# A macaron encoder trunk on one core: merged gate/up exits, P of two head groups through DRAM, a fourth seven-product chunk, and q, k ahead of V

## The chip, the cores and the metric

The kernel runs on one core of a Trainium2 chip. The metric is the device time of one execution in microseconds (us), from the first to the last activity on the core. Beside it stand views of one profiled execution of the kernel before. The engines are the tensor engine (PE, with its weight loads shown as PEld), the vector engine (DVE), the scalar engine (ACT), GpSimd (POOL) and the sync engine (SP), which here only issues DMAs.

## The reference

The input x is 256 rows (frames) of 1024. Two layers follow each other, and each is three residual blocks:

```python
for i in range(DEPTH):                                  # 2
    h = rmsnorm(x, ffn1_norm[i])
    x = x + 0.5 * swiglu(h, ffn1_w_gate[i], ffn1_w_up[i], ffn1_w_down[i])      # 1024 -> 2816 -> 1024
    h = rmsnorm(x, mix_norm[i]); proj = h @ w_in[i]     # q_s, k_s, v_s (768 each), q_m (256)
    ...                                                 # attention, see below
    x = x + concatenate([o_s, o_m]) @ w_out[i]
    h = rmsnorm(x, ffn2_norm[i])
    x = x + 0.5 * swiglu(h, ffn2_w_gate[i], ffn2_w_up[i], ffn2_w_down[i])
```

with swiglu(h) = (silu(h @ w_gate) * (h @ w_up)) @ w_down. In layer 0, o_s is causal chunked attention of 12 heads of 64 with a learned relative bias (chunks of 64 frames, and with 256 frames every earlier chunk is in reach). In layer 1 it is differential attention of 6 heads, softmax(q1 k1) - lambda softmax(q2 k2), with rotary embedding and a norm of the result. o_m is 4-head attention into a memory of 256 rows. q and k of every head are normalised. All data are float32.

## The kernel before

**Tiling.** Rows are two blocks tb of 128; features lie in tiles of 128. A product runs on the tensor engine as three matmuls of a rounded and a rest part (float32r): hi x hi, hi x lo, lo x hi (`dense`, lines 555, 558, 561). So each weight chunk is loaded by DMA into a raw buffer of 128 x 2048, ACT writes hi (L378, a cast) and the vector engine lo = raw - hi (L398). There are 3 raw buffers and 4 hi/lo buffers, so weights are split some chunks ahead.

**Stages.** FFN 1, mixer, FFN 2 of layer 0, then of layer 1. In an FFN the 2816 hidden columns are 11 groups of 256; a group needs two weight chunks (g, c), and its gate and up columns share one PSUM bank of 512 for each tb. `evac` ends a group: silu on ACT (L741), a multiply (L744) and a 32 x 32 block transpose (L752) on the vector engine, for each tb; then hb goes to DRAM and comes back re-ordered as hr, and is split into hi and lo (ht). Two groups of each FFN (`PAIR`) are computed as a pair by seven block products instead of eight (Strassen's way), with sums of weight blocks made by the vector engine (L390, wsum), each in four tiles of 512. The down projection runs over 11 chunks c into four accumulator banks. An ordinary chunk is 8 dense products, 24 matmuls. A chunk listed in `SEVEN` is 7 products, 21 matmuls: four sums of weight blocks, seven hi/lo splits instead of four, and sums of the left side (`seven_forms`, L791 to L804). Four of the seven products go to banks m of their own, which `seven_sums` adds to x at the end. The first such chunk of a stage takes two hi/lo buffers; the others take one, and half of x's own tiles as a guest, of which there is room for one. The last three chunks run tb by tb, each followed by `finish`, which updates x.

```python
SEVEN = {(0, 1): (), (0, 2): (1, 4, 7), (1, 1): (1, 4, 7), (1, 2): (1, 3, 5, 7)}
```

**Mixer.** Five blocks of 512 columns of w_in are projected (`proj`, 48 matmuls each): q and k of head group 0, V of groups 0 and 1, q and k of group 1, q and k of group 2, then the rest of V and the memory q. A group is four heads. `qk_evac` norms the heads (in layer 1 also rotates them), transposes q and k on the tensor engine and splits them. Eight units (group, tb) then do attention; group 3 is the memory. At most three units run at once (`tokens`): a unit takes its token before its scores and gives it back when its output stands in oT. A unit computes scores S, the softmax P, P's transpose and AV. P is transposed on the tensor engine (`p_transpose`, ptp, L591) and copied from PSUM by ACT (L1520): one 128 x 128 transpose for each head at tb = 0, two at tb = 1. In layer 0 the q halves are transposed with a flipped identity, and P likewise, because the bias is read from DRAM in reversed row order. The output projection (`outp`) takes groups 0 and 1 for both tb, then groups 2 and 3 tb by tb.

**Order.** Every engine works through its own instruction list in order, and semaphores make it wait. The lists are written by a planner, `Flow`, while the program is built: threads (generators) yield estimated times or conditions, and `flow.pe`, `flow.act`, `flow.dve` add estimated durations (`T_MM` a matmul, `T_TR` a transpose, `HOP` the way from one engine to another). The estimates decide the order of instructions and nothing else; on the chip only the real dependencies hold. PSUM is eight banks, given out by a counter (`Slots`). SBUF work buffers are 12 of 4 KB a partition (g4) and 19 of 2 KB (g2). Weights and hb/hr use SP's DMA queue; one earlier step (`prep_dram`) turns x through DRAM on ACT's queue.

## Time and profile before

| | |
|---|---|
| median of 3 runs | 946.02 us (945.81 to 946.78) |
| the profiled execution's own time | 945.89 us |
| its span, first to last instruction | 944.1 us |
| DMA | 206.13 MB, mean 218 GB/s |

The span is 1.8 us shorter than the time of the same execution. Stages by the first tensor instructions, in us of the span: FFN 1 to 180, memory keys and values and mixer 0 to 308.7, FFN 2 to 477, FFN 1 of layer 1 to 661, mixer 1 to 765.5, FFN 2 to the end. In a row of a group of instructions stand line, engine, operation, what is written from what is read, shapes and count, then busy us and mean ns of one, then the idle time of the engine just before them with what ended it. In a row of the timeline stand start and duration in us. In a row of stretches stand the stretch, its length, then busy us and count of PE, PEld, DVE, ACT and POOL, the granted clock of the tensor engine (1.00 is full), the DMA share and GB/s. In a row of DMAs stand count, size and the median time from issue to landing.

### The profile page before, as it was taken

What the parts mean: (1) busy time and instruction counts of PE and PEld (TensorE: products, weight loads), DVE (VectorE), ACT (ScalarE), POOL (GpSimd) and SP (SyncE); (2) the same over time, 40 slices, a digit from 0 to 9 for tenths busy, and PEclk for the clock granted to TensorE, in tenths of its full rate; (3) what the DMA queues carried; (4) which work ended last, traced back from release to release, by engine and by line L of the source; (5) the groups of instructions that cost most, each with busy time, mean ns of one, the idle gap of its engine ahead of it and who ended that gap; (6) DMA issues with size and microseconds to landing.
All of it is one profiled execution on the core that took longest, in us unless ns stands there. A gap on an engine that the chain in (4) does not pass through costs nothing. (4 is left out here: it accounts for less than half of the span.)

```text
span 944.1 us, 13356 instructions
## 1 busy us (share of the span) xinstructions
PE 938.1 (99%) x4469; PEld 772.6 (82%) x4469; DVE 830.6 (88%) x1506; ACT 592.5 (63%) x1129; POOL 107.2 (11%) x160
## 2 busy tenths in 40 slices
PE   9999999999999999999999999999999999999998
PEld 7888888888878888888888888888887788888886
DVE  6989888899886998988788998896989899998995
ACT  6656676677685756656555656664777765665671
POOL 0000028651210000000000000000334100000000
PEclk9999999999999999999999999999999999999999
DMA  9876899588425477887746588775632367689561
GB/s 299 261 245 197 262 365 336 203 275 275 148 91 178 133 237 228 258 292 239 242 157 219 192 257 262 256 249 169 223 120 70 126 222 223 198 269 315 182 217 47
DMA packets 172606, 206.13 MB, mean 218 GB/s; under 512 B 10297, under 2 KB 147322, under 8 KB 172538
## 3 DMA queue, kind: packets, MB, share of 16 engines
q1 hardware_dynamic: 169530, 202.92, 66.8%
q10 hardware_dynamic: 3008, 2.37, 0.8%
q8 instruction: 35, 0.57, 0.3%
q14 instruction: 33, 0.27, 0.1%
HBM read 190.04 MB, written 15.20 MB: 217 GB/s over the span
## 5 line engine op out<-in xcount | busy, mean ns | idle before, releaser
L398 DVE TENSOR_TENSOR lo<-raw,hi 128x512 fp32r<-128x512 f32 (+1 forms) x466 | 392.2, 876 | 38.5 <-ACT hi L378 37.8
L378 ACT CAST hi<-raw 128x512 fp32r<-128x512 f32 (+1 forms) x465 | 332.4, 769 | 141.2 <-DMA raw<-in_ffn_w_up_dram 34.7
L558 PE MATMUL gu<-lo,xh 128*128 128x512 f32 x528 | 205.7, 390 | 0.6 <-DVE lo L1816 0.6
L555 PE MATMUL gu<-hi,xh 128*128 128x512 f32 x528 | 205.8, 390 | 0.0
L561 PE MATMUL gu<-hi,xl 128*128 128x512 f32 x528 | 205.6, 389 | 0.0
L558 PEld LDWEIGHTS gu<-lo,xh 128*128 128x128 f32 x528 | 99.2, 188 | 21.5 <-DVE lo L1816 1.0
L561 PEld LDWEIGHTS gu<-hi,xl 128*128 128x128 f32 x528 | 99.1, 188 | 20.7
L555 PEld LDWEIGHTS gu<-hi,xh 128*128 128x128 f32 x528 | 99.3, 188 | 20.4
L561 PE MATMUL acc<-hi,ht 128*128 128x512 f32 x270 | 105.6, 391 | 0.0
L555 PE MATMUL acc<-hi,ht 128*128 128x512 f32 x270 | 105.1, 389 | 0.0
L558 PE MATMUL acc<-lo,ht 128*128 128x512 f32 x270 | 105.1, 389 | 0.0
L378 ACT CAST hi<-wsum 128x512 fp32r<-128x512 f32 x83 | 48.7, 618 | 26.8 <-DVE wsum L390 22.3
L558 PE MATMUL pj<-lo,xh 128*128 128x512 f32 x160 | 63.7, 398 | 0.0
L561 PE MATMUL pj<-hi,xl 128*128 128x512 f32 x160 | 63.6, 397 | 0.0
L555 PE MATMUL pj<-hi,xh 128*128 128x512 f32 x160 | 63.5, 397 | 0.0
L741 ACT ACTIVATE sil<-gu,xr 128x256 f32<-128x256 f32 x72 | 33.8, 471 | 42.9 <-PE gu L561 41.3
L558 PEld LDWEIGHTS acc<-lo,ht 128*128 128x128 f32 x270 | 50.7, 188 | 10.6
L561 PEld LDWEIGHTS acc<-hi,ht 128*128 128x128 f32 x270 | 50.7, 188 | 10.4
L555 PEld LDWEIGHTS acc<-hi,ht 128*128 128x128 f32 x270 | 50.7, 188 | 10.3
L598 POOL TENSOR_TENSOR xr<-v,nhalf 128x1 f32<-128x1 f32 x12 | 8.6, 720 | 435.0 <-DVE v L596 435.0
L398 DVE TENSOR_TENSOR lo<-wsum,hi 128x512 fp32r<-128x512 f32 x83 | 53.5, 681 | 0.0
L744 DVE SCALAR_TENSOR_TENSOR h<-gu,xr,sil 128x256 f32<-128x256 f32 x72 | 34.4, 478 | 7.2 <-ACT sil L741 6.7
(250 smaller groups left out, 1531.9 us busy)
## 6 DMA issues: line engine op xcount, KB each, us to landing
raw<-in_ffn_w_down_dram SPq DMA_DIRECT2D x176, 256.0 KB, 4.4
raw<-in_ffn_w_gate_dram SPq DMA_DIRECT2D x81, 512.0 KB, 4.2
raw<-in_ffn_w_up_dram SPq DMA_DIRECT2D x81, 512.0 KB, 5.4
raw<-in_w_in_dram SPq DMA_DIRECT2D x32, 512.0 KB, 5.4
hd<-hb SPq DMA_DIRECT2D x44, 256.0 KB, 4.8
hr<-hd SPq DMA_DIRECT2D x44, 256.0 KB, 4.7
raw<-in_w_out_dram SPq DMA_DIRECT2D x8, 1024.0 KB, 4.9
raw<-in_w_mem_kv_dram SPq DMA_DIRECT2D x4, 1024.0 KB, 6.1
```

The costliest lines, as they stand in the source:

```text
L378: nc.scalar.copy(out=it.part(0, q, w), in_=src())
L398: nc.vector.tensor_sub(it.part(1, q, w), src(), it.part(0, q, w).bitcast(F32))
L555: nc.tensor.matmul(out=ps, lhsT=xh, rhs=wh, start=start, stop=False)
L558: nc.tensor.matmul(out=ps, lhsT=xh, rhs=wl, start=False, stop=False)
L561: nc.tensor.matmul(out=ps, lhsT=xl, rhs=wh, start=False, stop=stop)
L598: nc.gpsimd.tensor_tensor(out=dst, in0=v[:, :n], in1=nhalf[:, :n], op=ALU.pow)
L741: nc.scalar.activation(sil, ps[tb][:, 0:256], AF.Silu, scale=xt.r[tb])
L744: nc.vector.scalar_tensor_tensor(out=h, in0=ps[tb][:, 256:512], scalar=xt.r[tb], in1=sil, op0=ALU.mult, op1=ALU.mult)
```

## The change

Seven things change together.

1. *Exits of plain groups are merged.* The two banks of a group must be neighbours. Both silus write one tile, one multiply of 512 and one block transpose of 512 serve both tb, and both banks are given back together. The row scale r is left out of the multiply; 0.5 r (`rh`, one POOL instruction for each norm) takes the place of 0.5 wherever an FFN's result is added to x.
2. *PSUM is one tile of eight banks*, given out by a list (`Banks`) that knows which bank is free: the longest free one, or two neighbours.
3. *Weight sums of the pair* use two tiles of 1024 from g4 in place of four of 512 from g2.
4. *SEVEN* becomes (1, 3, 5, 7) in FFN 2 of layer 0 and FFN 1 of layer 1.
5. *P of groups 0 and 1 of mixer 0* goes through DRAM (`trip`): a block transpose on the vector engine, a write and a read, both issued on ACT's queue. AV reads the result where it lands. The flipped identity goes; the bias arrives row by row from an array laid out so.
6. *Mixer 1* projects q, k of groups 0, 1, 2, then V, then the last block.
7. *The planner's estimates* change, and `split_evac` issues the casts of k and q before their rests.

```diff
-T_MM = 0.216
-T_TR = 0.107
+T_S1, T_S3 = 0.0012, 0.0009
+T_AV1, T_AV2 = 0.127, 0.219
+HOP_E = 0.14
+T_MM = 0.2285
+T_TR = 0.09
...
-        return self.free[e] + HOP
+        return self.free[e] + HOP_E
...
+class Banks:
+    def __init__(self, tile):
+        self.tile, self.free, self.held = tile, list(range(8)), {}
...
+    def has_pair(self):
+        return lambda: any(b + 1 in self.free for b in self.free)
...
+    def take(self, shape):
+        b = self.free[0]
...
+    def take_pair(self):
+        age = self.free.index
+        b = min((b for b in self.free if b + 1 in self.free), key=lambda b: max(age(b), age(b + 1)))
+        return self._hold(self.tile[:, b:b + 2, :], (b, b + 1))
...
-    FULL = 600.0
+    FULL = 620.0
...
-    SEVEN = {(0, 1): (), (0, 2): (1, 4, 7), (1, 1): (1, 4, 7), (1, 2): (1, 3, 5, 7)}
+    SEVEN = {(0, 1): (), (0, 2): (1, 3, 5, 7), (1, 1): (1, 3, 5, 7), (1, 2): (1, 3, 5, 7)}
...
-            it.sums = [(at_(x, j), at_(y, j)) for j in range(4)]
-            it.units = [((lambda j=j: it.t[j]), j, 1, j) for j in range(4)]
+            it.room = g4
+            at_ = lambda v, j: it.own(2 * j, 2, v) if isinstance(v, int) else (lambda: v.t[j])
+            it.sums = [(at_(x, j), at_(y, j)) for j in range(2)]
+            it.units = [((lambda j=j: it.t[j]), 2 * j, 2, j) for j in range(2)]
...
+        nc.gpsimd.tensor_scalar(out=xt.rh[tb], in0=xt.r[tb], scalar1=0.5, scalar2=None, op0=ALU.mult)
...
-                nc.vector.scalar_tensor_tensor(out=xs[tb][:, sl], in0=acc.ps[tb][hf], scalar=0.5, in1=xs[tb][:, sl],
+                nc.vector.scalar_tensor_tensor(out=xs[tb][:, sl], in0=acc.ps[tb][hf], scalar=rh[tb], in1=xs[tb][:, sl],
...
-                nc.vector.scalar_tensor_tensor(out=h, in0=ps[tb][:, 256:512], scalar=xt.r[tb], in1=sil,
-                                               op0=ALU.mult, op1=ALU.mult)
...
+                    nc.scalar.activation(sil[:, tb], ps[:, tb, 0:256], AF.Silu, scale=xt.r[tb])
+                    t = flow.act(256)
+                yield t
+                h = g2.take([P, 2, 2, 4, 32], F32, "h")
+                nc.vector.tensor_mul(h.rearrange("p t f b i -> p t (f b i)"), ps[:, :, 256:512], sil)
+                t = flow.dve(512, 0.06)
                 g2.give()
+                banks.give(ps)
+                hb = g2.take([P, 4, 2, 2, 32], F32, "hb")
...
+                nc.vector.transpose(out=hb.rearrange("p b t f j -> p (t f) b j"),
+                                    in_=h.rearrange("p t f b i -> p (t f) b i"))
...
-                flow.until(banks.has(2))
-                open_[g] = [bank(f"gu{tb}", (P, 512)) for tb in range(2)], [None, None]
+                flow.until(banks.has_pair())
+                open_[g] = banks.take_pair(), [None, None]
...
-                nc.sync.dma_start(out=b, in_=bass.AP(tensor=a_rel_bias.tensor, offset=4 * c * 384,
-                                                     ap=[[1, P], [384, 4], [1, SEQ]]))
+                nc.sync.dma_start(out=b, in_=a_rel_bias[:, 4 * c:4 * c + 4, :])
...
+        def trip(src, n):
+            yield g2.has()
+            m = n // P
+            xb = g2.take([P, 4, m, 32], F32, "tb")
+            nc.vector.transpose(out=xb.rearrange("p b m j -> p m b j"), in_=src.rearrange("p (m i b) -> p m b i", b=4, i=32))
+            t = flow.dve(n, n / 1200.0)
+            g2.give()
+            yield t + 0.1
+            d = dram.tile([4, 32, 4, m * 32], F32, tag=f"td{m}", name="td", bufs=4)
+            nc.scalar.dma_start(out=d.rearrange("a i b x -> (a i) (b x)"), in_=xb.rearrange("p b m j -> p (b m j)"))
...
+            yield flow.now + 4.5
+            g2.give()
+            yield g2.has()
+            r = g2.take([P, 4, m * 32], F32, "tr")
+            nc.scalar.dma_start(out=r, in_=d.rearrange("a i b x -> (i b) a x"))
...
+            yield flow.now + 5.0
+            return r.rearrange("p a (m j) -> p m a j", j=32)
...
+        def carried(src, nk, pts, e):
+            r = yield from trip(src.rearrange("p a b -> p (a b)"), 2 * nk)
+            pts[e] = r.rearrange("p (a b) c j -> p a b c j", a=2)
...
-                pt, t = yield from p_transpose(pes[e][0], nk, bias_t is not None)
-                pts.append(pt)
+                if grp < 2 and typ_a:
+                    flow.spawn(carried(pes[e][0], nk, pts, e))
+                    continue
+                pt, t = yield from p_transpose(pes[e][0], nk)
+                pts[e] = pt
+            yield lambda: None not in pts
...
-        proj(0, qk_evac(0))
-        flow.until(g4.has(2))
-        take_v()
-        proj(1, v_evac)
-        proj(2, qk_evac(1))
-        proj(3, qk_evac(2))
-        proj(4, vq_evac)
+        for i, k in enumerate(("q0", "v", "q1", "q2", "w") if typ_a else ('q0', 'q1', 'q2', 'v', 'w')):
+            todo[k](i)
```

More of the change, by code (lines that the diff above doesn't have):

```diff
@@ L384, in split_lo @@
             if it.sums:
-                yield lambda: all(r.raw is not None for r in it.raws) and g2.left >= it.takes + 2
+                yield lambda: all(r.raw is not None for r in it.raws) and it.room.left >= it.takes + (2 if it.room is g2 else 0)
                 yield max(r.arrive for r in it.raws)
-                it.t += [g2.take([P, 512], F32, "wsum") for _ in range(it.takes)]
+                w = 512 if it.room is g2 else 1024
+                it.t += [it.room.take([P, w], F32, "wsum") for _ in range(it.takes)]
                 for j, (x, y) in enumerate(it.sums):
@@ L401, in split_lo @@
             raw_left[0] += it.frees
-            g2.give(it.gives)
+            it.room.give(it.gives)
     def k4(t):
@@ L535 @@
         plan[l, "in"] = []
-        for blk in WI:
+        for blk in WI if l == 0 else WI1:
             ids = []
@@ L588, in two_phases, with turn @@
         return t
-    def turn(dst, src, flipped=False):
-        nc.tensor.transpose(out=dst, in_=src, identity=flip if flipped else ident)
+    def turn(dst, src):
+        nc.tensor.transpose(out=dst, in_=src, identity=ident)
         return flow.pe(T_TR)
@@ L710, in finish @@
                 nc.vector.tensor_add(xs[tb][:, sl], acc.ps[tb][hf], xs[tb][:, sl])
-            banks.give()
+            banks.give(acc.ps[tb][hf])
             yield flow.dve(512)
@@ L755, in evac @@
+                t = flow.dve(512, 0.1)
                 g2.give()
@@ L1433, in run @@
                     else:
-                        nc.scalar.copy(out=f.rearrange("p a b c -> p (a b) c"), in_=tp)
+                        nc.scalar.copy(out=a4(f.rearrange("p a b c -> p (a b) c")), in_=tp)
                         t = flow.act(512)
-                    banks.give()
+                    g2.give() if far else banks.give(tp)
                     yield t
@@ L1780 @@
     wb = bank("warm")
-    banks.give()
     def warm(n):
@@ L1826 @@
     nc.vector.tensor_copy(gcol[:, 0:16], tp[:, 0, :16])
-    banks.give()
+    banks.give(tp)
     warm(2)
@@ L1844 @@
     warm(4)
+    banks.give(wb)
     flow.now = 5.35
```

256 lines of the change are left out of this document (154 added, 102 removed).

## The prediction

> **What bounds the kernel now.** I read the page first, then the order of the tensor queue, then the stretches by stage.
>
> ```profile
> span 944.1 us, 13356 instructions
> PE 938.1 (99%) x4469; PEld 772.6 (82%) x4469; DVE 830.6 (88%) x1506; ACT 592.5 (63%) x1129; POOL 107.2 (11%) x160
> PEclk9999999999999999999999999999999999999999
> ```
>
> The tensor engine is covered for 938.1 of 944.1 us at the full granted clock. Covered is not the same as at its peak, so the second view is the timeline of the tensor queue, here in a down stage of layer 0.
>
> ```profile
> 430.20 0.39 PE L555 MATMUL acc<-hi,ht 128*128 128x512 f32 x1
> 430.43 0.39 PE L558 MATMUL acc<-lo,ht 128*128 128x512 f32 x1
> 430.66 0.39 PE L561 MATMUL acc<-hi,ht 128*128 128x512 f32 x1
> 430.88 0.39 PE L555 MATMUL acc<-hi,ht 128*128 128x512 f32 x1
> 431.11 0.39 PE L558 MATMUL acc<-lo,ht 128*128 128x512 f32 x1
> 431.34 0.39 PE L561 MATMUL acc<-hi,ht 128*128 128x512 f32 x1
> ```
>
> One matmul of 512 columns starts every 1.14 / 5 = 0.228 us, although each is shown 0.39 us long. A matmul less is therefore worth about 0.227 us. That this pace holds is seen in the stretches: the next rows run from the first matmul of chunk 0 to the first of chunk 8 of three down stages (FFN 2 of layer 0, FFN 1 of layer 1, FFN 2 of layer 1).
>
> ```profile
> 426.30:467.80 41.50, 41.50 (x184) 34.36 (x184) 35.51 (x62) 27.16 (x51) 0.00 (x0) 1.00 0.79 248
> 603.00:644.50 41.50, 41.50 (x184) 34.35 (x183) 35.41 (x63) 27.72 (x53) 0.00 (x0) 1.00 0.76 242
> 883.20:924.00 40.80, 40.80 (x182) 33.78 (x181) 39.99 (x74) 28.36 (x55) 0.00 (x0) 1.00 0.53 171
> ```
>
> The code gives the first two 5 x 24 + 3 x 21 = 183 matmuls and the third, which has four seven-product chunks already, 4 x 24 + 4 x 21 = 180; 41.50 / 183 = 40.80 / 180 = 0.227 us. So the feed-forward stages run without a gap, and only removed matmuls can shorten them. The third row also shows four seven-product chunks at full pace with the vector engine busy 39.99 of 40.80 us.
>
> The mixers are less clean. These stretches go from the last projection to the first matmul of the next stage, in mixer 0 and mixer 1.
>
> ```profile
> 274.90:308.70 33.80, 33.80 (x232) 27.09 (x230) 25.24 (x56) 22.66 (x56) 1.01 (x1) 1.00 0.46 148
> 730.10:765.50 35.40, 35.01 (x220) 27.93 (x219) 30.60 (x70) 24.03 (x65) 4.45 (x4) 1.00 0.55 173
> ```
>
> Mixer 1 issues 12 records fewer and takes 1.6 us more. With some 0.07 us for a record of the attention (an AV of 24 records below takes 1.53), its tail holds about 1.6 + 0.8 = 2.4 us of real waiting for attention results. I take those 2.4 us as all that a better order there can win.
>
> **The fourth seven-product chunk.** The tuples of chunks go from (1, 4, 7) to (1, 3, 5, 7) in the first two rows above. Each changed stage gains one chunk of 7 x 3 = 21 matmuls in place of 8 x 3 = 24: 3 x 0.227 = 0.68 us, twice 1.36 us; the row at 883.20 against the others shows just this step, 0.70 us. Its cover is the vector engine, which gets per stage four block sums, three more lo splits, four form sums and larger splits of the left side:
>
> ```profile
> L390 DVE TENSOR_TENSOR wsum<-raw,wsum 128x512 f32<-128x512 f32 x52 | 34.2, 678 | 0.2
> L398 DVE TENSOR_TENSOR lo<-wsum,hi 128x512 fp32r<-128x512 f32 x83 | 53.5, 681 | 0.0
> L791 DVE TENSOR_TENSOR sf<-hr 128x128 f32<-128x128 f32 x20 | 5.6, 281 | 0.0
> L804 DVE TENSOR_TENSOR h<-sf,h 128x512 fp32r<-128x512 f32 x10 | 6.9, 686 | 0.2
> ```
>
> 4 x 0.68 + 3 x 0.68 + 4 x 0.28 + about 0.7 = 6.6 us more, on 35.5 busy: 42.1 in a stretch of 40.8. The overhang of 1.3 us has to come from work done ahead. The merged exits just before make that: I cost the chunk's own stall at nothing, at most 1.3 us a stage if no work lies ahead.
>
> **The merged exits.** Nine groups of each FFN are evacuated by one multiply and one block transpose of 512 in place of two of 256, and the row scale moves from the multiply to the final x update (0.5 becomes 0.5 times the scale, made once by a POOL instruction long before it is read).
>
> ```profile
> L744 DVE SCALAR_TENSOR_TENSOR h<-gu,xr,sil 128x256 f32<-128x256 f32 x72 | 34.4, 478 | 7.2 <-ACT sil L741 6.7
> L752 DVE STREAM_TRANSPOSE hb<-h 128x256 f32<-128x256 f32 x88 | 38.4, 437 | 0.0
> L710 DVE TENSOR_TENSOR x<-acc,x 128x512 f32<-128x512 f32 x8 | 5.4, 686 | 3.3 <-PE acc L561 3.3
> L636 DVE STREAM_TRANSPOSE xb<-x 128x512 f32<-128x512 f32 x4 | 4.4, 1094 | 0.0
> L398 DVE TENSOR_TENSOR lo<-raw,hi 128x1024 fp32r<-128x1024 f32 x162 | 193.4, 1213 | 11.1 <-ACT hi L378 10.7
> ```
>
> The multiply: 2 x 0.478 = 0.96 before, one of 0.69 from PSUM (L710's row). The transpose: 0.87 before; after it between twice 0.437 and L636's 1.09, whose source is strided as this one is not; I take 0.80. Saved: 0.27 + 0.07 = 0.34 us a group, between 0.05 and 0.45, so some 3 us for the nine groups of a stage. The pair sums, in tiles of 1024 in place of 512, save 2 x 0.68 - 1.21 = 0.15 us for each of 8 sums and 8 splits, 2.4 us a stage. All of it is vector time under a saturated tensor queue: worth nothing by itself, but it is the 5 us of head start that the fourth chunk needs. What it costs is banks: both banks of a group stay taken until the one multiply is done, and the two must be neighbours. I cost that at nothing, because eight banks hold two open groups with four to spare; the other end is the last rival.
>
> **P of groups 0 and 1 by DRAM (mixer 0).** 24 tensor transposes and 8 scalar copies go; 8 vector transposes and 16 DMAs issued on ACT's queue come. The tensor queue of group 0:
>
> ```profile
> 237.98 0.39 PE L558 MATMUL pj<-lo,xh 128*128 128x512 f32 x1
> 238.22 0.38 PE L591 MATMUL ptp<-flip,pe 128*128 128x128 f32 x2
> 238.35 0.48 PE L561 MATMUL pj<-hi,xl 128*128 128x512 f32 x1
> 238.66 0.39 PE L555 MATMUL pj<-hi,xh 128*128 128x512 f32 x1
> ...
> 240.50 0.60 PE L591 MATMUL ptp<-flip,pe 128*128 128x128 f32 x4
> 240.86 0.48 PE L558 MATMUL pj<-lo,xh 128*128 128x512 f32 x1
> 241.17 0.40 PE L561 MATMUL pj<-hi,xl 128*128 128x512 f32 x1
> ```
>
> Two transposes cost 0.13 us, and the matmul behind them starts its successor after 0.31 instead of 0.227: 0.22 us. Four cost 0.36 + 0.08 = 0.44 us. A group has two visits of each kind: 1.32 us, two groups 2.64 us. That is the gross gain.
>
> Its price is time to arrive. The rows are the end of group 1's softmax, its AV, and the first matmul of the output projection that reads group 1; then the DMAs of the two round trips that the kernel makes already.
>
> ```profile
> 266.43 1.14 DVE L1571 TENSOR_SCALAR pe<-pe,rs 128x256 f32<-128x256 f32 x4
> 272.58 1.53 PE L1590 MATMUL AV<-PT,V 128*64 128x128 f32 x24
> 284.13 0.48 PE L555 MATMUL acc<-hi,oT 128*128 128x512 f32 x1
> xd<-xb ACTq DMA_DIRECT2D x4, 256.0 KB, 3.2
> xr<-xd ACTq DMA_DIRECT2D x4, 256.0 KB, 5.6
> hd<-hb SPq DMA_DIRECT2D x44, 256.0 KB, 4.8
> hr<-hd SPq DMA_DIRECT2D x44, 256.0 KB, 4.7
> ```
>
> P is ready at 267.6; two vector transposes (2 x 1.09) reach 269.8; write and read take 3.2 + 5.6 = 8.8 or 4.8 + 4.7 = 9.5: 278.6 to 279.3. AV is 1.5 us and its two evacuations about 0.8: usable at 281 to 281.6. Group 1 is wanted at 284.1 - 2.6 = 281.5, if nothing else moves. So it arrives just in time. Late next is group 1's part of the output projection; the second DMA waits at the head of ACT's queue for the first, and behind it stand the exponentials of group 2. Between no stall and the whole 2.6 us given back I take 0.5, near the lower end since the planner can put other scores in between. Reading P through 32-element pieces as the moving operand stands in no row; AV's 1.53 us could at most double, twice 1.5; an ACT cast of the same pieces takes 0.62 us, as one of plain rows does, so I take zero:
>
> ```profile
> L775 ACT CAST ht<-hr 128x512 fp32r<-128x512 f32 x34 | 20.9, 618 | 24.8 <-DMA hr<-hd 24.8
> L378 ACT CAST hi<-wsum 128x512 fp32r<-128x512 f32 x83 | 48.7, 618 | 26.8 <-DVE wsum L390 22.3
> ```
>
> Group 0's P is turned at 240.50 for the last time, so its trip ends near 240.5 + 2.2 + 9.5 = 252 and is wanted at 274.9: hidden under projections. The flipped identity goes with its replacement by a bias laid out row by row in DRAM, loaded in as many DMAs of the same size far ahead: nothing.
>
> **q and k ahead of V (mixer 1).** The five blocks are the same matmuls, so only the 2.4 us of waiting can move. All scores can start some 11 us earlier, but AV then waits for V, now the fourth block, and three units with a token stand there until it comes. From V's end there are still 11 us of the last block and 11 us of output projection of groups 0 and 1 to hide the rest. Between winning all 2.4 and losing 2.4 more I take 1.0 won, because a unit of group 2 began its scores only behind all projections, and the queue waited for them:
>
> ```profile
> 733.09 1.54 PE L1506 MATMUL S<-k,q 64*128 64x256 f32 x12 [0.26 <-ACT PT L1520]
> ```
>
> In the new order its q and k are there 11 us sooner.
>
> **The planner's numbers.** Estimated durations (a matmul 0.2285 for 0.216, a hop 0.14 for 0.22) alter only the order in which instructions are written. The lead that the new order gives can't be read from this trace; I take zero, and 1 us to either side for the range.
>
> **Sum**, against the profiled execution (945.89 us with its span of 944.1; the median of the three runs is 946.02, 0.1 more): 1.36 + 2.64 - 0.5 + 1.0 = 4.5 us. 945.9 - 4.5 = 941.4 us.
>
> **The rivals.** *The mixers give it back* (944.5): the two ends above, P late by its 2.6 us and the new order of mixer 1 worth nothing, leave 945.9 - 1.4. For it: P's slack is 0.5 us at best. Against it: scores and AVs of groups 2 and 3 can stand in between.
>
> *The waits vanish too* (938.9): 945.9 - 1.36 - 2.64 - 2.4 and about 0.6 of the small waits of mixer 0.
>
> *The vector engine binds* (945.4): then matmuls removed win nothing in the FFNs, and each changed down stage loses its overhang of 1.3 us: 945.9 - 2.64 + 0.5 - 1.0 - 0 + 2.6 = 945.4. For it: 39.99 of 40.80 us in the third row above. Against it: the pace of 0.227 us in that very row. The Trainium skill's page "Perfetto Trace Analysis", section "Identifying the Most-Contended Engine", holds that the busy share of the matmul row is no good measure and that of the weight loads is; by that, 82% here, the tensor engine would have room and this rival would hold. The trace does not agree: 34.36 us of loads for 184 matmuls are 0.187 us in each slot of 0.227, 82% with no slot free; by the rule the time is this rival's 945.4, by the trace it is the forecast's.
>
> *No two neighbouring banks* (954.6, the slower side): during the pair's seven products, four single banks are out beside a group's pair. Where no neighbours are free when a group opens, the queue waits for an exit, two silus, estimated at the 0.48 of L744, and the multiply: 2 x 0.48 + 0.69 = 1.65 us. It decides from the first group opened while the free banks lie apart; at two groups a stage, four stages: 8 x 1.65 = 13.2 us on top of 941.4.
>
> **How the numbers follow.** Forecast 0.56, mixers give it back 0.22, vector engine 0.08, banks 0.07, waits vanish 0.07. The range takes in the ends of the forecast's terms, the second and the last case and most of the first rival: 938.8 to 945.5. A measurement of this kernel can tell 0.2%, 1.9 us. Faster by more: 0.56 + 0.07 and half of the 0.22, 0.74. Slower by more: the banks and a part of the vector case, 0.09. The same: 0.17.
>
> **What would show it.** Right: acc<-hi,ht falls from 270 to 254 records, transposes of P from 86 to 62, the stretches of both changed down stages measure 40.8 us, the tail of mixer 1 is shorter than 35.4 us at about the same records. P late shows as a gap in front of AV or of the first acc of group 1, with a DMA or ACT as releaser. Banks show as waits of the first gu matmul of a group for L744's successor. A down stage above 41.5 us, or a mixer 0 not at least 1.5 us shorter, makes the forecast wrong.

## The result and the profile after

The changed kernel takes 952.66 us (median of 6 executions, 950.31 to 953.67) against 946.06 (945.81 to 946.78): 1.0064 of the time before, with an interval of 1.0051 to 1.0077. The forecast of 941.4 us missed by 11 us and had the sign wrong. The profiled execution took 950.31 us, the fastest of the six, so the traces below explain 4.4 us of the loss; the spread of the others is taken up with the runs.

The page of the changed kernel: span, busy times, granted clock, and the chain of waits that ended last.

```profile
span 948.5 us, 13199 instructions
PE 938.4 (99%) x4439; PEld 770.5 (81%) x4439; DVE 832.9 (88%) x1404; ACT 587.0 (62%) x1097; POOL 110.6 (12%) x170
PEclk9999999989999999999999999999999999999999
PE 83%; DVE 6%; POOL 5%; DMA 2%; issue 2%; ACT 1%; SPq 0%; ACTq 0%; DVEq 0%
L597 PE MATMUL banks<-hi,ht 128*128 128x512 f32 x254 | 99.1, 390 | 0.0
```

Two things are new. One slice of the granted clock is an 8, and POOL, which computes next to nothing, has 5% of the chain, some 47 us. The 254 records of the down product are as forecast. Which stage lost is read from the stretches (columns as in the prediction), each from the first matmul of a stage to the first of the next. Before, in this order: memory keys and values, mixer 0, the down product of FFN 2 of layer 0, that of FFN 1 of layer 1, mixer 1.

```profile
185.60:207.30 21.70, 21.70 (x97) 18.00 (x96) 19.40 (x38) 16.81 (x34) 15.77 (x28) 1.00 0.85 267
207.30:308.70 101.40, 101.40 (x618) 82.28 (x617) 84.14 (x228) 73.21 (x182) 14.72 (x9) 1.00 0.53 173
426.10:485.40 59.30, 59.30 (x269) 49.06 (x268) 49.43 (x84) 33.13 (x61) 0.54 (x1) 1.00 0.66 209
602.80:662.10 59.30, 59.30 (x269) 49.08 (x268) 49.24 (x87) 34.12 (x66) 0.44 (x1) 1.00 0.64 205
662.10:765.50 103.40, 102.94 (x579) 82.79 (x578) 94.37 (x202) 73.60 (x196) 31.83 (x28) 1.00 0.47 151
```

The same five after:

```profile
185.60:214.10 28.50, 25.56 (x97) 19.96 (x96) 25.49 (x57) 17.95 (x38) 5.35 (x8) 0.88 0.84 278
214.10:313.80 99.70, 99.08 (x594) 80.09 (x593) 88.80 (x225) 70.28 (x175) 17.06 (x13) 1.00 0.65 211
431.20:489.80 58.60, 58.60 (x266) 48.43 (x265) 55.94 (x98) 35.83 (x67) 0.79 (x2) 1.00 0.61 199
607.20:665.80 58.60, 58.60 (x266) 48.50 (x265) 55.91 (x100) 37.17 (x74) 1.42 (x2) 1.00 0.61 199
665.80:770.20 104.40, 102.83 (x579) 82.22 (x578) 95.01 (x206) 73.22 (x196) 32.97 (x30) 1.00 0.46 152
```

The two down stages give 0.7 us each, mixer 0 gives 1.7, mixer 1 takes 1.0: together 2.1 us gained; the last FFN gives 0.3 more (178.3 us for 178.6). The stage of memory keys and values (called the k/v stage below) takes 28.5 us in place of 21.7 for the same 97 matmuls. These 6.8 us are the result, and the prediction has no line about this stage. Part of what it multiplies (memh, the hi blocks of the memory) is made on ACT in the 30 us before it begins. So the next view is ACT's timeline of the changed kernel (start, duration, in brackets the idle time before and its releaser).

```profile
167.74 1.31 ACT L1213 ACTIVATE memh<-mr,gcol 128x256 fp32r<-128x256 f32 x3
177.69 0.26 ACT L1368 ACTIVATE ropew<-ropew 128x64 f32<-128x64 f32 x1 [8.64 <-POOL ropew L1337]
179.07 0.26 ACT L1369 ACTIVATE ropew<-ropew 128x64 f32<-128x64 f32 x1 [1.12 <-POOL ropew L1337]
179.35 1.28 ACT L1112 ACT_TABLE_LOAD   x1
180.75 0.49 ACT L1213 ACTIVATE memh<-mr,gcol 128x256 fp32r<-128x256 f32 x1
```

ACT executes in the order of its list. At 169 us it comes to the Sin of the rotary tables, which mixer 1 reads from 666 us on. The Sin waits 8.64 us for a chain of some 90 short instructions on POOL, and the memory's last hi blocks and the weight casts stand behind it. The last load of memory weights, which needs a raw buffer that these casts help to free, is issued at 186.7 us, and at 172.9 in the kernel before. There the Sin stood later in ACT's list and met no wait:

```profile
204.09 1.28 ACT L1298 ACT_TABLE_LOAD   x1
205.39 0.26 ACT L1298 ACTIVATE ropew<-ropew 128x64 f32<-128x64 f32 x1
```

What the late casts do to the tensor engine, in its timeline and in one stretch (length, PE busy and count, granted clock, DMA share, GB/s) of the changed kernel:

```profile
188.11 0.39 PE L603 MATMUL banks<-hi,meml 128*128 128x512 f32 x1
190.36 0.50 PE L597 MATMUL banks<-hi,memh 128*128 128x512 f32 x1 [1.86 <-ACT hi L417]
191.91 0.80 PE L600 MATMUL banks<-lo,memh 128*128 128x512 f32 x1 [1.05 <-DVE lo L438]
192.51 0.63 PE L603 MATMUL banks<-hi,meml 128*128 128x512 f32 x1
192.93 0.63 PE L597 MATMUL banks<-hi,memh 128*128 128x512 f32 x1
```

```profile
191.90:198.00 6.10, 6.09 (x14) 0.50 0.97 328
```

From 188.11 to 190.36 and from 190.36 to 191.91 the queue stands: less one slot of 0.227 each, 2.0 and 1.3 us. Then for 6.1 us the granted clock is 0.50 and a matmul starts every 0.42 us (192.51 to 192.93), 0.2 more than at the full clock: 14 x 0.2 = 2.8 us. 2.0 + 1.3 + 2.8 = 6.1 of the 6.8 us.

Why the Sin stands so early, by an estimate: in the planner's time a step of the rotary chain costs 0.25 us plus the wait behind an engine, which the change takes from 0.22 to 0.14, so 0.39 in place of 0.47. The two most frequent of its lines, after, up to 180 us:

```profile
L1335 POOL TENSOR_SCALAR ropew<-ropew 128x64 f32<-128x64 f32 x20 | 11.7, 584 | 1.7
L1337 POOL TENSOR_TENSOR ropew<-ropew 128x64 f32<-128x64 f32 x20 | 7.5, 374 | 1.6
```

With the idle time before them, (11.7 + 1.7 + 7.5 + 1.6) / 40 = 0.56 us a step. Over 90 steps the plan is ahead of the chip by about 90 x 0.17 = 15 us now, and was by 90 x 0.09 = 8 us. The new number is the worse estimate just where the chain is long.

### The profile page after: what moved, and what is told of

The parts are those of the page before. It is cut to its first block, busy times and chain, and to the rows that moved or that the text cites. A ratio compares the mean times of both kernels' runs of the same rounds, so it can differ in the third digit from the quotient of the medians.

```text
span 948.5 us, 13199 instructions
## 1 busy us (share of the span) xinstructions
PE 938.4 (99%) x4439; PEld 770.5 (81%) x4439; DVE 832.9 (88%) x1404; ACT 587.0 (62%) x1097; POOL 110.6 (12%) x170
## 4 chain that ended last, share of the span: by engine, by line
PE 83%; DVE 6%; POOL 5%; DMA 2%; issue 2%; ACT 1%; SPq 0%; ACTq 0%; DVEq 0%
PE banks L600 25%; PE banks L597 25%; PE banks L603 25%; DVE lo L438 2%; PE banks L620 2%; PE banks L633 2%; PE banks L1605 1%; POOL ropew L1335 1%; PE banks L626 1%; PE banks L1697 1%; POOL ropew L1337 1%; DMA xr<-xd 1%; POOL ropew L1351 1%; DMA xd<-xb 1%; DMA raw<-in_ffn_w_down_dram 1%
## 5 line engine op out<-in xcount | busy, mean ns | idle before, releaser
L600 PE MATMUL banks<-lo,xh 128*128 128x512 f32 x736 | 287.9, 391 | 0.5 <-DVE lo L1928 0.5
L597 PE MATMUL banks<-hi,xh 128*128 128x512 f32 x736 | 288.1, 391 | 0.0
L603 PE MATMUL banks<-hi,xl 128*128 128x512 f32 x736 | 287.6, 391 | 0.0
L600 PEld LDWEIGHTS banks<-lo,xh 128*128 128x128 f32 x736 | 138.3, 188 | 29.2 <-DVE lo L1928 0.9
L597 PEld LDWEIGHTS banks<-hi,xh 128*128 128x128 f32 x736 | 138.4, 188 | 28.5
L603 PEld LDWEIGHTS banks<-hi,xl 128*128 128x128 f32 x736 | 138.3, 188 | 28.6
L597 PE MATMUL banks<-hi,ht 128*128 128x512 f32 x254 | 99.1, 390 | 0.0
L603 PE MATMUL banks<-hi,ht 128*128 128x512 f32 x254 | 99.1, 390 | 0.0
L600 PE MATMUL banks<-lo,ht 128*128 128x512 f32 x254 | 98.9, 390 | 0.0
L603 PEld LDWEIGHTS banks<-hi,ht 128*128 128x128 f32 x254 | 47.7, 188 | 9.9
L597 PEld LDWEIGHTS banks<-hi,ht 128*128 128x128 f32 x254 | 47.7, 188 | 9.8
L438 DVE TENSOR_TENSOR lo<-wsum,hi 128x1024 fp32r<-128x1024 f32 (+1 forms) x53 | 52.3, 1008 | 2.7 <-ACT hi L417 2.0
```

The source lines that it names most:

```text
L438: nc.vector.tensor_sub(it.part(1, q, w), src(), it.part(0, q, w).bitcast(F32))
L597: nc.tensor.matmul(out=ps, lhsT=xh, rhs=wh, start=start, stop=False)
L600: nc.tensor.matmul(out=ps, lhsT=xh, rhs=wl, start=False, stop=False)
L603: nc.tensor.matmul(out=ps, lhsT=xl, rhs=wh, start=False, stop=stop)
```

## The experiments

Lengths in us from the first matmul of a stage to the first of the next, of each run's profiled execution. "Base" is the changed kernel with the old wait behind an engine (0.22). Each ratio is taken to the executions of the kernel before that ran beside that kernel; their medians lie between 946.06 and 946.75 us.

| run | time | ratio to before, interval | k/v | mixer 0 | FFN 2 down | FFN 1 down | mixer 1 |
|---|---|---|---|---|---|---|---|
| before | 946.06 | | 21.7 | 101.4 | 59.3 | 59.3 | 103.4 |
| changed | 952.66 | 1.0064 (1.0051 to 1.0077) | 28.5 | 99.7 | 58.6 | 58.6 | 104.4 |
| Sin later | 950.52 | 1.0046 (1.0028 to 1.0064) | 28.0 | 101.9 | 58.5 | 58.6 | 104.5 |
| before, new numbers | 965.29 | 1.0192 (1.0177 to 1.0207) | 39.8 | 100.9 | 59.2 | 59.3 | 105.7 |
| old order of mixer 1 | 953.04 | 1.0070 (1.0054 to 1.0086) | 30.9 | 99.7 | 58.5 | 58.6 | 106.5 |
| Sin later, old order | 952.80 | 1.0073 (1.0054 to 1.0091) | 26.0 | 102.0 | 58.5 | 58.5 | 106.6 |
| three old numbers | 946.74 | 1.0003 (0.9993 to 1.0012) | 21.8 | 98.3 | 60.3 | 58.6 | 103.9 |
| old matmul number | 960.10 | 1.0141 (1.0124 to 1.0158) | 31.4 | 103.1 | 60.3 | 58.6 | 106.4 |
| base: old wait | 944.48 | 0.9979 (0.9970 to 0.9988) | 21.7 | 98.8 | 58.5 | 58.6 | 105.8 |
| three old numbers, old order | 947.12 | 1.0009 (0.9999 to 1.0018) | 21.8 | 98.3 | 60.3 | 58.6 | 104.3 |
| base, transposes later | 942.74 | 0.9964 (0.9951 to 0.9977) | 21.8 | 98.7 | 58.6 | 58.5 | 104.5 |
| base, P on tensor engine | 947.20 | 1.0008 (0.9998 to 1.0017) | 21.7 | 102.0 | 58.5 | 58.6 | 105.8 |
| base, three seven-product chunks | 945.53 | 0.9996 (0.9987 to 1.0006) | 21.8 | 98.8 | 59.3 | 59.2 | 105.8 |
| base, old order | 942.18 | 0.9956 (0.9942 to 0.9971) | 21.8 | 98.8 | 58.6 | 58.6 | 103.8 |
| base, old order, transposes later | 945.74 | 0.9995 (0.9985 to 1.0004) | 21.8 | 98.7 | 58.5 | 58.6 | 107.6 |
| before, new wait | 953.58 | 1.0079 (1.0064 to 1.0094) | 25.9 | 101.2 | 59.3 | 59.2 | 104.7 |
| base, old order, exits halved | 942.11 | 0.9957 (0.9942 to 0.9972) | 21.7 | 98.8 | 58.7 | 58.6 | 103.8 |
| base, old order, Sin early | 951.35 | 1.0056 (1.0040 to 1.0073) | 30.2 | 98.8 | 58.8 | 58.6 | 103.8 |
| old order, wait 0.18 | 956.02 | 1.0103 (1.0088 to 1.0118) | 30.8 | 102.5 | 58.5 | 58.7 | 105.9 |
| old order, wait 0.30 | 944.89 | 0.9986 (0.9977 to 0.9996) | 21.8 | 100.7 | 58.6 | 58.5 | 105.2 |

**The Sin later.**

```diff
         sn = fa
+        yield flow.now + 16.0
         nc.scalar.activation(sn, acc, AF.Sin, scale=S2PI)
```

> The changed kernel with one line more: the rope thread waits 16 us of planned time ahead of its two Sin, so that ScalarE gets them behind the memory's last hi blocks and not ahead of them. Nothing else is edited; the same tables are computed. Theory A (the k/v stage lost 6.8 us because the Sin stood in ScalarE's in-order queue ahead of the memory's hi blocks and waited 8.64 us for GpSimd; the half clock that followed is a consequence of TensorE's waits): the k/v stage falls from 28.5 us to 21 to 23 us, no stretch of granted clock 0.5 is left in it, and the profiled span falls from 948.5 to about 942. Theory B (the stage lost its time to something else in the change, the merged exits or the order in which weights are split, and the Sin waits in a shadow): the stage stays at 27 us or more and the span over 947.

The Sin now meets no wait, and the stage is still 28.0 us long. By the text above this speaks for theory B; ACT's timeline of this run, and then five rows of the chain that ended last (start, duration), say what it is.

```profile
185.92 0.38 ACTq L692 DMA_DIRECT2D xr<-xd  x1
186.39 0.62 ACT L417 CAST hi<-raw 128x512 fp32r<-128x512 f32 x1 [6.44 <-DMA xd<-xb]
```

```profile
178.53 7.37 DMA xd<-xb
188.70 1.28 ACT L1369
190.92 1.28 ACT L1409
193.21 0.61 DVE lo L438
193.87 0.80 PE banks L600
```

Two things hold the casts up now. The read of x back from DRAM, a DMA that ACT issues, stands ahead of them and goes out at 185.92, when the write of x, issued at 178.53, has landed after 7.4 us. And the Sin stands among the casts: its table load (L1369, 1.28 us) and that of the exponential which the program places behind it (L1409, 1.28 us) come ahead of casts, and VectorE's next rest waits behind the result of that exponential. The tensor engine stops twice, for 0.7 and 2.7 us, and half clock follows. So my theory was too narrow: to move the Sin by 16 us of plan takes its wait away, and not its place among entries that the tensor engine needs sooner.

**The planner's numbers alone, on the kernel before.**

```diff
-T_MM = 0.216
-T_TR = 0.107
+HOP_E = 0.14
+T_MM = 0.2285
+T_TR = 0.09
-        return self.free[e] + HOP
+        return self.free[e] + HOP_E
```

(The scores' numbers as in the change, too.)

> The kernel before with nothing of the change but the planner's numbers: a matmul at 0.2285 us, a transpose at 0.09, the wait behind an engine 0.14 instead of 0.22, and the scores' numbers. Every part of the work is that of the kernel before. Theory A (the numbers alone put the Sin ahead of the memory's hi blocks): the Sin again waits several us for GpSimd, the k/v stage grows from 21.7 to 26 to 29 us, and the time rises by 4 to 7 us over the kernel before, to 950 to 953. Theory B (the loss needs the merged exits or the new sums): the stage stays within 1 us of 21.7 and the time within 1.5 us of 946.

18.5 us slower, the k/v stage 39.8 us. Waits of ACT, then of PE, in that stage: line waiting, what for, us in total, times, longest.

```profile
ACT ropew L1299 <- POOL ropew L1268: 11.3, 1, 11.3
PE kv L556 <- ACT hi L379: 8.0, 1, 8.0
PE kv L562 <- DVE meml L1154: 4.1, 1, 4.1
```

No merged exit, no trip of P through DRAM and no new chunk is in this kernel. The numbers suffice, and the direction of theory A holds; its size, 4 to 7 us, does not.

**The second mixer's order, and both edits.**

```diff
-        for blk in WI if l == 0 else WI1:
+        for blk in WI:
-        for i, k in enumerate(("q0", "v", "q1", "q2", "w") if typ_a else ('q0', 'q1', 'q2', 'v', 'w')):
+        for i, k in enumerate(("q0", "v", "q1", "q2", "w")):
```

> The changed kernel with the second mixer's blocks in the old order (first q,k block, V, two q,k blocks, V and memory q). Theory A (the new order delays the scores of the later units behind late q,k rotations and costs that mixer a net 1.0 us): the second mixer goes from 104.4 us back to 103.4 or a little less, its projections from 71.7 to about 68, and the span from 948.5 to about 947.5; the k/v stage stays at 28.5. Rival (the order itself is worth the 1 us of gain that was forecast and the planner's numbers cost the mixer 2 us): the second mixer stays at 104.4 or grows by up to 1 us.

> The changed kernel with both edits: the Sin 16 us of plan later and the second mixer's blocks in the old order. Theory A for both: the k/v stage at 21 to 23 us and the second mixer at about 103.4, so a span of 940.5 to 941.5 and a time of 942 to 943.5, faster than the kernel before. If only the Sin counts: 943.5 to 944.5. If neither: over 948.

With the changed kernel's numbers the old order costs mixer 1 2.1 us, twice (104.4 to 106.5, 104.5 to 106.6): the rival was right in its direction here, and its 1 us was too small. Both edits together come out as in the last line of their text, over 948 us. These pairs also say where the spread of executions sits. The tensor and scalar lists of the changed kernel and of the first of these two are the same up to mixer 1, and yet their k/v stages took 28.5 and 30.9 us; the pair with the later Sin 28.0 and 26.0. A stage that waits varies by 2 us; in all runs without waits there it measures 21.7 to 21.8.

**Which number.** The three old numbers, the old matmul alone, the old wait alone, and the three with the old order of mixer 1:

```diff
-HOP_E = 0.14
-T_MM = 0.2285
-T_TR = 0.09
+HOP_E = 0.22
+T_MM = 0.216
+T_TR = 0.107
```

> The changed kernel with the planner's old numbers for a matmul (0.216 us), a transpose (0.107) and the wait behind an engine (0.22); all parts of the work are those of the change. Theory C (the numbers carry the whole loss: with a matmul planned shorter than the 0.227 us that it takes, the plan runs ahead of the chip and every split, Sin and readback is ordered with room to spare; the true number takes this room away): the k/v stage falls from 28.5 us to 21 to 23, no granted clock under 0.9 in any slice, and the span from 948.5 to 939 to 942, so a time of 941 to 944, faster than the kernel before. Rival D (the merged exits or the new sums make the splits late, the numbers only add): the stage stays at 25 us or more and the time over 947.

> The changed kernel with the planner's matmul at the old 0.216 us alone; transpose 0.09 and wait behind an engine 0.14 as in the change. If the matmul's number is what takes the room away (theory C, my first guess): k/v stage 21 to 24 us, span 940 to 944. If it is the wait behind an engine: stage 26 us or more, span 946 or more.

> The changed kernel with the planner's wait behind an engine at the old 0.22 us alone; matmul 0.2285 and transpose 0.09 as in the change. If the matmul's number is what takes the room away: k/v stage 26 us or more, span 946 or more. If it is the wait: stage 21 to 24 us, span 940 to 944. If both are needed, both single edits stay over 945.

> The changed kernel with the old numbers for matmul, transpose and wait, and the second mixer's blocks in the old order too. Theory C gives the same k/v stage as with the old numbers alone, 21 to 23 us; the second mixer (projections and tail, 104.4 us in the changed kernel, 103.4 before) at 103 to 104. If the order forecast stands (the new order gains 1.0 us once the numbers are the old ones), this one is 0.5 to 1.5 us slower than the run with old numbers alone; if the new order costs, it is 0.5 to 1.5 us faster.

My guess was wrong: the old matmul number with the new wait is worse than the change (960.10), while the old wait alone brings the k/v stage to 21.7 and the kernel to 0.9979 of the time before. In that run the first read of x stands ahead of ACT's casts as well, but its write has landed early:

```profile
177.80 0.34 ACTq L685 DMA_DIRECT2D xd<-xb  x1
180.54 0.48 ACTq L692 DMA_DIRECT2D xr<-xd  x1
182.87 1.14 ACT L417 CAST hi<-raw 128x512 fp32r<-128x512 f32 x2 [3.05 <-PE banks L603]
```

The read goes out 2.7 us behind the write, and the casts wait for a buffer that PE frees, as in the kernel before, and not for a round trip. Here the write was issued 0.6 us ahead of the sync engine's last 1 MB load of memory weights (178.37); with the Sin later it was issued 1.0 us behind that load (177.51), and its first packets moved at 182 us. That the load is what held it up is likely, and no run here tests it. The k/v stage of the run with three old numbers is 21.8 as theory C has it, but its time is 2.7 us over that theory's range. With the old matmul number the down stage of FFN 2 is 60.3 us in all three runs, and with the old wait beside it the gate/up stage ahead of it is 120.7 us for 117.4 in the base; PE waits in the gate/up stage for the split of x, and in the down stage for a weight's rest:

```profile
PE banks L620 <- ACT xh L706: 1.7, 1, 1.7
PE banks L600 <- DVE lo L438: 1.0, 1, 1.0
```

**The wait alone on the kernel before; the Sin alone on the base.**

```diff
-        return self.free[e] + HOP
+        return self.free[e] + 0.14
```

> The kernel before with one number changed: the wait behind an engine 0.14 us instead of 0.22. If this number alone makes the loss: the k/v stage grows from 21.8 to 26 us or more, granted clock 0.5 stands in it behind the waits, and the time rises by 4 us or more over the kernel before. If it needs the other numbers or the change's other parts: stage 21.5 to 23 us, time within 2 us of the kernel before.

```diff
-            yield flow.pool(0.25)
+            yield flow.pool(0.17)
```

(all steps of the rotary chain, on the base with the old order of mixer 1)

> The changed kernel with the old wait and the old order in the second mixer (span 940.1, k/v stage 21.8, Sin behind the memory's last hi block), and the rope's steps on GpSimd planned at 0.17 us instead of 0.25, so that the Sin is planned early again, ahead of the memory's last hi blocks. If the Sin's place in ScalarE's queue is enough by itself: ScalarE waits 5 us or more in front of it, the k/v stage grows to 24 to 29 us with granted clock 0.5 in it, and the span to 942.5 or more. If the loss needs the readback of x in front of the splits as well: stage within 1 us of 21.8.

Both came out on the first side, though not in every figure: the stage is 25.9 us for 26 or more in the first, and in the second 30.2, over the 24 to 29 of its text, at full clock where the text has 0.5. One number makes the kernel before 0.8% slower: its k/v stage 25.9 us, and 2.5 us more in its first gate/up stage, where PE waits for weights' rests (`lo`, 0.6 and 0.4 us in its largest waits; the kernel before has none there). And the Sin's early place is enough by itself, since only the planned length of the rotary steps differs from the 942.18 us kernel:

```profile
ACT ropew L1368 <- POOL ropew L1337: 9.8, 1, 9.8
PE banks L600 <- DVE lo L438: 4.2, 4, 1.9
PE banks L597 <- ACT hi L417: 2.4, 1, 2.4
```

The k/v stage has 8.4 us more, 6.6 of them in these waits, and no other stage moved by over 0.2.

**A lead, or a place?** The base with the old order, wait 0.18 and 0.30.

```diff
-HOP_E = 0.22
+HOP_E = 0.18
```

> The changed kernel with the old order in the second mixer and the planner's wait behind an engine at 0.18 us, halfway between the two values run so far (0.14: k/v stage 30.9 us, time 953; 0.22: 21.8 us, time 942.2). The Sin is planned ahead of the memory's last hi blocks, as at 0.14. If the Sin's place decides: ScalarE waits 5 us or more in front of it, k/v stage 24 to 31 us, time 945 to 952. If the number buys room gradually: k/v stage 22 to 24 us, time 942 to 945.

> The same with the wait at 0.30 us, larger than the old one. The Sin is planned behind the memory's hi blocks. If a larger number only buys room, at no cost in the k/v stage: stage 21.5 to 22.2 us, no wait of TensorE in it; the second mixer may move by 2 us to either side, since the order there is decided anew: time 940 to 945. If too large a number delays the splits themselves: a stage over 23 us or matmuls of the feed-forward stages that wait, time over 946.

It is the place. In seven of these kernels the Sin stands so early that it waits for POOL, 7.2 to 12.8 us (changed, old order, old matmul number, wait 0.18, Sin early, and the kernel before with all new numbers or the new wait), and their k/v stages take 25.9 to 39.8 us. At 0.18 the Sin stands ahead of the memory's last hi blocks and waits 10.7 us, and the stage is as long as at 0.14 (30.8 and 30.9); at 0.22 and 0.30 it stands behind them, and the stage is 21.8. The time at 0.18 is over both texts' ranges: the mixers are longer too (102.5 and 105.9, for 98.8 and 103.8 at 0.22).

**The parts of the change, on the base.** P of groups 0 and 1 on the tensor engine again, then three seven-product chunks again:

```diff
-                if grp < 2 and typ_a:
+                if False:
```

> The same base, with all of P transposed on TensorE again (nothing by DRAM). The prediction's sum has 2.64 us less tensor work for P by DRAM and 0.5 given back for P that arrives late: the first mixer goes from 98.8 to 100.4 to 101.5 us and the span from 942.0 to 943.6 to 944.7; nothing else moves. If P by DRAM is not what shortens the first mixer: within 0.7 us of 942.0.

```diff
-    SEVEN = {(0, 1): (), (0, 2): (1, 3, 5, 7), (1, 1): (1, 3, 5, 7), (1, 2): (1, 3, 5, 7)}
+    SEVEN = {(0, 1): (), (0, 2): (1, 4, 7), (1, 1): (1, 4, 7), (1, 2): (1, 3, 5, 7)}
```

> The same base, with three seven-product chunks in place of four in the two down stages that the change touches. Each of the two stages, 58.6 us with four, grows by 0.7 (the prediction has 0.68): the span from 942.0 to 943.4, give or take 0.3. If the fourth chunk's gain comes back elsewhere: less than 0.7 in all.

Mixer 0 of the base and in the first, then FFN 2's down stage in the second:

```profile
207.10:305.90 98.80, 98.80 (x593) 80.31 (x593) 89.53 (x237) 70.08 (x174) 14.97 (x10) 1.00 0.65 213
207.50:309.50 102.00, 101.94 (x618) 82.79 (x618) 83.54 (x229) 72.58 (x182) 14.39 (x10) 1.00 0.54 176
```

```profile
423.40:482.70 59.30, 59.30 (x269) 49.10 (x268) 50.04 (x83) 33.14 (x61) 0.78 (x2) 1.00 0.61 199
```

P by DRAM is worth 3.2 us of mixer 0 (102.0 against 98.8), more than the 2.64 gross of the prediction and over its text here; the medians differ by 2.7. The base's mixer 0 has PE covered for all of its 98.80 us, so no matmul waits for P. AV reads P in pieces of 32 elements at no cost: 16 of its matmuls start within 0.82 us from either layout. The fourth chunk is worth 0.8 and 0.6 us in its stages; the medians differ by 1.05.

**Exits halved** (base with the old order):

```diff
-                nc.vector.tensor_mul(h.rearrange("p t f b i -> p t (f b i)"), ps[:, :, 256:512], sil)
+                for tb in range(2):
+                    nc.vector.tensor_mul(h[:, tb].rearrange("p f b i -> p (f b i)"), ps[:, tb, 256:512], sil[:, tb])
```

(the block transpose likewise)

> The changed kernel with the old wait and the old order in the second mixer (span 940.1), and the merged exit's one product and one transpose over both token blocks made as two each of half the size, still from two neighbouring banks. The prediction took the merged exits at no change of the end: VectorE about 13 us busier, span within 0.5 us of 940.1. If VectorE's time does bind in the gate/up stages (117.4 us each): one or more of the three rises by over 0.5 us.

942.11 against 942.18, no stage moved by more than 0.1 us. VectorE is busy 835.9 us for 832.1, on its page and on that of the run with whole exits: 3.8 us for 36 groups, 0.1 us a group. That is not the prediction's 0.34, since the halves here are a plain multiply and a transpose of 0.42 us each, and the kernel before has 0.478 and 0.437. Against the kernel before, the rows of the whole exits decide it:

```profile
L816 DVE STREAM_TRANSPOSE hb<-h 128x512 f32<-128x512 f32 x36 | 25.4, 704 | 0.1
L810 DVE TENSOR_TENSOR h<-banks,sil 128x512 f32<-128x512 f32 x36 | 24.6, 684 | 0.2 <-ACT sil L806 0.2
```

2 x 0.478 + 2 x 0.437 - 0.684 - 0.704 = 0.44 us a group, at the upper end of the 0.05 to 0.45 forecast.

**Mixer 1 on the base.** The old order, and more planned time ahead of the transposes of the rotated block, with the new order and with the old one:

```diff
-                    if typ_a:
-                        yield flow.now + 2.0
+                    yield flow.now + (2.0 if typ_a else 1.0)
```

> The same base, with the second mixer's blocks in the old order (V second). With the changed kernel's own numbers the new order was worth 2.1 us in that mixer (106.5 against 104.4), with all old numbers 0.5 us (104.3 against 103.8). If the new order gains: second mixer 106.3 to 108 us here, span 942.5 to 944.2. If it costs with these numbers: second mixer 104 to 105.3, span 940.2 to 941.5.

> The changed kernel with the wait behind an engine at 0.22 us again, and in the second mixer 1.0 us of planned time more between the rotated q,k block and the four transposes that TensorE makes of it, so that matmuls with their operands at hand stand ahead of them. The base for all four runs of this set is the run with the old wait alone: span 942.0, k/v stage 21.8, first mixer 98.8, second mixer 105.8 us. If TensorE's waits ahead of these transposes (1.1 us on it and 2.1 us on its weight loads in that run) are the second mixer's loss: second mixer 102.5 to 104, span 939 to 940.5. If they only stand where another wait would: second mixer 105 or more, span over 941.5.

> The changed kernel with the old wait of 0.22 us and the old order of the second mixer's blocks (span 940.1, second mixer 103.7), and 1.0 us of planned time more ahead of the transposes of rotated q,k there. With the new order that last edit took 1.3 us from the second mixer. If it acts on its own: 102.3 to 103 us, span 938.8 to 939.5. If the old order already gives TensorE other work in that place: within 0.5 us of 103.7.

On the base the new order loses 2.0 us, where it gained 2.1 with the changed kernel's numbers and 0.4 with all old ones. Its waits there are in front of the transposes of rotated blocks, first the base, then the kernel with the later transposes:

```profile
PE banks L633 <- DVE m L1479: 1.1, 3, 0.4
```

```profile
PE banks L633 <- DVE pe L1742: 1.3, 3, 0.8
```

The named wait goes and 1.3 us are won, to 104.5, between what the two sides of its text expect; transposes of P wait in its stead. With the old order the same edit loses 3.8 us (103.8 to 107.6), the largest wait, 1.6 us, again in front of P. Neither text held for that run. Mixer 1 lay between 103.4 and 107.6 us in these kernels, with the same products in all. What decides it I can't say.

The kernel with the old wait and the old order of mixer 1 beats both: 942.18 us, 0.9956 of the time before (0.9942 to 0.9971).

## Why the prediction was wrong

- **The planner's numbers: the step that failed.** "Estimated durations ... alter only the order in which instructions are written ... I take zero, and 1 us to either side". That they alter only the order is right, and the order of ACT's list is worth 6.8 us in the profiled execution (18.5 us in the median of the kernel before with all the numbers). A bound was there to be had: POOL's rows for the rotary chain, which in the kernel before too take 0.58 us a step (15 + 15 instructions, busy 9.1 + 5.9 us, idle before them 1.2 + 1.2) where the new plan would say 0.39, and the question which entry of an in-order list waits for that chain. The prediction asks it for the new DMAs on ACT's queue in mixer 0 and not for the entries already there.
- **The fourth seven-product chunk: right**, 0.7 us in each stage for 0.68. VectorE is busy 55.9 of 58.6 us there and did not bind; that rival is out.
- **P by DRAM: right in mechanism, too small.** Net 2.64 - 0.5 = 2.14 against 3.2 measured with the old wait. No wait for P stands in mixer 0 there; the 0.5 was not due. The bound of twice for AV came from no row, and AV did not change.
- **q, k ahead of V: not a constant.** Forecast 1.0 won. Measured 2.1 won, 0.4 won or 2.0 lost, by the planner's numbers; in the changed kernel itself mixer 1 lost 1.0 against before. Its tail is shorter, as forecast (32.7 us for 35.4), but the projections are longer (71.7 for 68.0).
- **Merged exits: right at zero**, also when halved again. The vector time saved is 0.44 us a group for 0.34, because the transpose of 512 takes 0.70 us for 0.80. No wait for two neighbouring banks appears; the rival on the slower side had the wrong place.
- **The sum without the failed step.** The base with the old order has a span of 940.1 us, 4.0 under the kernel before, with mixer 1 0.4 longer; for the chunks and P by DRAM 1.36 + 2.14 = 3.5 was forecast.
- **Open.** Of the changed kernel's 6.6 us at the median its profiled execution shows 4.4. The rest was not traced; the pairs above show the k/v stage varying by 2 us, which is the likely place. Mixer 1's 1.0 us is not settled either.

## What to carry to other kernels

Where a planner writes the instruction lists, its estimates are part of the kernel: time a change of them by itself, on the old kernel, before judging anything that comes with it. In an in-order list look for the entries that nobody needs soon and that wait for a slow producer (a long chain of short instructions, a DMA's round trip), since everything behind them is late by their wait; such an entry belongs behind the urgent ones, and a chain's estimate needs the gap between its instructions as well as their duration. The gain that is a count of matmuls removed from the busy engine held to 0.1 us a stage in this case, that of the transposes was larger than its count by 0.6 us; the gain argued from order changed its sign with the planner's numbers.

## What the runs showed of the hardware

The tensor clock can halve after a wait that is short. In the kernel before with the new wait a single stop did it (its wait row, then two stretches: length, PE busy and count, granted clock):

```profile
PE kv L558 <- DVE lo L398: 1.9, 1, 1.9
```

```profile
189.94:193.36 3.42, 1.56 (x7) 1.00 0.55 162
193.36:196.77 3.41, 3.41 (x9) 0.50 0.51 153
```

With the Sin early on the base, stops of 2.6 and 1.2 us with one matmul between them left it whole:

```profile
186.71:190.12 3.41, 1.58 (x7) 1.00 0.73 243
190.12:193.53 3.41, 1.87 (x7) 1.00 0.91 318
```

So the same few us of waiting cost 0 more, or 2.8 as in the changed kernel. The Trainium skill's page "TensorE: Matmul & The Clock Gate", section "Part 1: The HAM clock gate (the "warmup" mystery)", says that the gate passes four or eight of eight pulses, that it falls back after an idle window of some 3.4 us, and that the window runs freely. The rows agree with the half, 0.50, and the clock records of the traces with a window that runs freely. Between the first full clock and the last matmul there are nine half periods in eight traces; they last 3.41, 6.83 or 10.24 us, and each begins a whole number of 3.413 us after the first full clock of its trace. The stretches above are cut on that grid. Counting as stop what lies between two starts over 0.5 us apart, less 0.227, the windows just ahead of a half clock hold 2.02 to 3.19 us of stop, and no other window at full clock holds over 1.99, in all twenty traces. The first case above is the 2.02; in the second the grid splits the stop of 2.6 us, and 1.99 and 1.81 us fall into the two windows. So the measurement differs from the page in one point: a window need not be idle throughout, 2.0 of its 3.4 us were enough here. That this is the limit is read from these traces alone.

The other surprise is the cost of small work on POOL: 0.37 to 0.58 us for an instruction over 128 x 64 elements, the rows of the rotary chain above, and 0.56 us from one to the next.
